# A diffusion layer on one core: the recurrence's chain as one stream of whole rows instead of two, ranked first

## The chip, the core and the metric

The kernel runs on 1 core of a Trainium2 chip. The metric is device time in microseconds (us), the median of several runs.

## What is computed

One layer over 2048 latent tokens and 256 context tokens, width 1024: modulated RMS norm, one input projection, two groups of heads side by side (neighbourhood attention and a bidirectional recurrence), an output projection, then a gated FFN. The change lies in the recurrence:

```python
def step(s, inp):
    r_t, w_t, k_t, v_t, a_t, b_t = inp
    sa = jnp.einsum('bhvk,bhk->bhv', s, a_t)
    s = s * w_t[:, :, None, :] + sa[..., None] * b_t[:, :, None, :] + v_t[..., None] * k_t[:, :, None, :]
    return s, jnp.einsum('bhvk,bhk->bhv', s, r_t)
```

It runs over 8 heads of width 64 in both directions, first over the context from a zero state, then over the latents from the state that the context leaves.

## The kernel before

Three stages follow each other. `phase1` projects all tokens and writes the recurrence's operands to DRAM. `phase2` runs attention and the recurrence side by side. `phase4` does the output projection (L1446), with the recurrence's norm and gate for each of 16 tiles of tokens just ahead of it (`TimeMixOutput.tile`, L1267 to L1283, and the transpositions L1404), and then the FFN.

In `phase2` the recurrence is cut into 36 chunks of 64 tokens per direction, two to each step `s` of 18, four to a block of two steps, so nine blocks. A pair of heads (`hp`, four of them) fills the 128 partitions, 64 each. The work of a block:

- `build` (L971) loads the operands of one step and one pair, multiplies them head by head (L1002) into one PSUM bank for each head, and spreads the result: the triangular system `lx` by ACT (L1008, two copies of 32 rows each), masked products `ga` and `gb` by DVE (L1010, L1014). Eight builds make a block. `lx` has two buffers, so the builds of block G wait for the chain of block G-2.
- `inverses` (L1042) solves the 32 systems of a block, one inverse per block: DVE transposes (L1053), POOL cuts the triangle (L1055), then DVE works through rows: single ones (L1067, L1069), then seven steps of four rows with a multiplication (L1076), a reduction (L1079) and an addition (L1080); DVE transposes back, and PE joins the halves (L1100, L1109).
- `lates` (L1019) transposes the operands that the end of a chunk needs (L1035, L1038).
- `chain` (L1160) carries the state `z` through one chunk: ACT and DVE copy it beside the loaded values (L1175, L1176), PE multiplies (L1180), ACT copies (L1184), PE multiplies by the inverse (L1188), ACT and DVE copy (L1172), PE multiplies (L1195), DVE adds the state (L1200) and scales it (L1212). From the third step on PE also forms the readout in the same bank (L1206 with 64 rows of one head, L1209 with all 128), ACT copies it (L1216) and SP stores it (L1134). There are two such chains, `g` = 0 and 1, with two pairs of heads each.

Attention runs in 64 tiles (`Attention.tiles` and `products`, L740 to L839): scores, softmax, transpositions, products with the values.

The order is made when the program is built. Every part is a generator that yields what it will occupy (`yield "run", ("ACT", 0.27)`) and what it waits for. `emit` (L862) keeps a clock for each engine and takes the part that can start first; among parts that can start at the same time a number decides, one for each stream:

```python
LATE = (60, 60, 60, -10, -10, 0, 0, 0, 60, 0)
key = (max(e[0], free.get(e[3][1][0], 0.0)), e[0] + LATE[e[1]], e[1])
emit(banks, chains(0), inverses(), chains(1), lates(0), lates(1), builds(0), builds(1), at.products(), at.tiles(),
```

The chains, the inverses and attention's tiles stand at 60. A scheduler then moves single instructions on each engine; `Run` (L48) pins a group of products to each other so that nothing comes between.

Of the kernel before, what the change touches and what calls it, by code (L numbers as in the profile page):

```python
# [93 lines left out]
def phase1(k):  # L94

    tc, nc, I = k.tc, k.nc, k.I
    with ExitStack() as ctx:
# [295 lines left out]
        def work_build(ops, hp, t0):  # L393
# [4 lines left out]
            for dd in range(2):  # L398
# [19 lines left out]
                nc.gpsimd.tensor_copy(k.pc[:, s0:s0 + 2, hp // 2, :, 2 * dd + hp % 2],  # L418
# [428 lines left out]
NU = 17  # L847
# [10 lines left out]
LATE = (60, 60, 60, -10, -10, 0, 0, 0, 60, 0)  # L858
# [53 lines left out]
def phase2(k):  # L912
# [4 lines left out]
    with ExitStack() as ctx:  # L917
# [9 lines left out]
        pch = [ps[6 + g].tile([P, 2, 4, 64], F32, name=f"pch{g}") for g in range(2)]  # L927
# [43 lines left out]
        def build(s, hp, w):  # L971
# [3 lines left out]
            if G > 1:  # L975
                yield "wait", ("chain", 2 * G - 3, 0), ("chain", 2 * G - 3, 1)
            if 4 * s + hp >= NU:
                yield "wait", ("chain", (4 * s + hp - NU) // 4, (4 * s + hp - NU) % 4 // 2)
# [16 lines left out]
            N = 128 if s > 1 else 64  # L995
            for h in range(2):
                z = []
                yield "get", z, 1
                yield "run", ("PE", 1.0)
                gp = z[0].rearrange("p (j t) -> p j t", j=4)  # L1000
                for j in range(4):
                    nc.tensor.matmul(gp[:, j, 0:N], bk[H[h], j], u.ga[H[h], h:3:2 - h, j, :] if s > 1 else  # L1002
                                     u.ga[H[h], h, j, :], start=True, stop=True)
                yield "run", ("ACT", -0.43), ("DVE", -0.34)
                ko = H[1 - h]
                for i in range(2):
# [12 lines left out]
        def lates(g):  # L1019

            for m in range(2 * NS):
                s, c = divmod(m, 2)
                if m > 1:
                    yield "wait", ("chunk", m - 2, g)
# [17 lines left out]
        def inverses():  # L1042
# [3 lines left out]
            for s in range(NS // 2):  # L1046
# [3 lines left out]
                lv = lu[:, :, 0:32]  # L1050
                x = cp.tile([P, 32, 32], F32, tag="lu", name="lu")
# [9 lines left out]
                red = cp.tile([P, 256], F32, tag="xt", name="red")  # L1061
# [74 lines left out]
        def chains(g):  # L1136

            z = ch.tile([P, 2, 2, 64], F32, tag=f"z{g}", name="z0", bufs=2)
            nc.gpsimd.memset(z, 0.0)
            if g:  # L1140
                load_v(0)
                yield "post", ("values", 0)
            yield "run", ("DMA", 2.2)
            for s in range(NS):
                yield "wait", ("inv", s // 2, 2 * g + 1)
                us = [U.pop((s, 2 * g + q)) for q in range(2)]
                for c in range(2):
                    m = 2 * s + c
                    yield "wait", ("values", m), ("late", m, g)
                    if g and m + 1 < 2 * NS:  # L1150
                        load_v(m + 1)
                        yield "post", ("values", m + 1)
                    z = yield from chain(s, c, g, z, us)
                    yield "post", ("chunk", m, g)
                yield "post", ("chain", s, g)

        dq = [(dd, q) for dd in range(2) for q in range(2)]
        kept = []

        def chain(s, c, g, z, us):  # L1160
            lx, j0 = LX[s // 2], 4 * (s % 2)
            zv = ZV[2 * s + c]
            tt = TT_.pop((2 * s + c, g))
            rp, up_ = pch[g][:, 0], pch[g][:, 1]
            gs = slice(P * g, P * g + P)

            def slot(h, dd, q):
                return zv[:, h, dd, P * g + 64 * q:P * g + 64 * q + 64]

            def keep():  # L1170
                for h, copy in ((0, nc.scalar.copy), (1, nc.vector.tensor_copy)):
                    copy(zv[H[h], h, :, gs], up_[H[h]].rearrange("p (d q) n -> p d (q n)", d=2))  # L1172

            yield "run", ("ACT", 0.27), ("DVE", 0.2)
# [521 lines left out]
```

## Time and profile before

| | us |
|---|---|
| median of 3 runs (3614.16 to 3624.52) | 3618.38 |
| the profiled execution | 3615.05 |
| its span | 3613.3 |
| PE busy in the span | 3433.7 (95%) |
| DVE, ACT, POOL busy | 2469.6, 1536.3, 1056.3 |

The span is the time from the first instruction to the last; the profiled execution's own time has 1.75 us around it. Busy is the time in which at least one instruction of the engine ran. `phase2` lies at 899 to 1988 us of the span. Products of fp32 operands have two records each in the trace.

### The profile page before, as it was taken

The numbers are of one execution on the slowest core, as the hardware profiler recorded it, in microseconds if no ns is written. First come the engines' busy times: TensorE is split into PE (matmuls) and PEld (weight loads), VectorE is DVE, ScalarE is ACT, GpSimd is POOL, SyncE is SP. The second block draws the span as 40 slices with busy tenths as digits, with TensorE's granted clock in tenths as the row PEclk, the third lists the DMA queues.
The fourth block names the chain that finished last, engine by engine and source line by source line (L and its number), as shares of the span: only waits on it lengthen the run. The fifth ranks groups of instructions, "written<-read, shape, count | busy, mean of one in ns | idle before, by whom it ended". The sixth has DMA issues, their size and how long they took to land. (4 is left out here: it accounts for less than half of the span.)

```text
span 3613.3 us, 66769 instructions
## 1 busy us (share of the span) xinstructions
PE 3433.7 (95%) x25202; PEld 2910.8 (81%) x25202; DVE 2469.6 (68%) x4570; ACT 1536.3 (43%) x3502; POOL 1056.3 (29%) x975
## 2 busy tenths in 40 slices
PE   7899999999889999999888999999899999899999
PEld 5787878889767677777676887888799999799998
DVE  7658786772675776667666674444877778777776
ACT  4524343442556566655433454323333334333332
POOL 3425543552000000000013243233433334433332
PEclk8999999999789899999866999999999999999999
DMA  7546666554544454444335455233422222412222
GB/s 238 158 146 201 188 185 190 166 165 123 160 121 129 117 145 140 124 132 123 93 91 154 141 193 170 94 96 102 140 65 70 71 70 72 162 62 71 71 70 68
DMA packets 461858, 458.52 MB, mean 127 GB/s; under 512 B 56656, under 2 KB 381664, under 8 KB 461536
## 3 DMA queue, kind: packets, MB, share of 16 engines
q1 hardware_dynamic: 461536, 454.25, 41.8%
q8 instruction: 199, 3.26, 0.4%
q14 instruction: 123, 1.01, 0.1%
HBM read 346.37 MB, written 107.75 MB: 126 GB/s over the span
## 5 line engine op out<-in xcount | busy, mean ns | idle before, releaser
L1317 ACT ACTIVATE w<-raw 128x512 fp32r<-128x512 f32 x440 | 270.4, 628 | 496.5 <-PE acc L1606 188.5
L1526 PE MATMUL acc<-ua,w 128*128 128x384 f32 x2464 | 469.1, 336 | 8.5 <-DVE h L1611 3.3
L1606 PE MATMUL acc<-w,fh 128*128 128x512 f32 x1408 | 437.5, 395 | 20.7 <-ACT fh L1317 8.4
L1318 DVE TENSOR_TENSOR w<-raw,w 128x512 fp32r<-128x512 f32 x308 | 280.5, 914 | 245.2 <-ACT w L1317 122.0
L1526 PEld LDWEIGHTS acc<-ua,w 128*128 128x128 f32 x2464 | 433.3, 189 | 11.8 <-DVE h L1611 3.7
L219 PE MATMUL acc<-u,wh 128*128 128x512 f32 (+3 forms) x1120 | 349.6, 392 | 11.7 <-ACT wh L209 5.6
L1606 PEld LDWEIGHTS acc<-w,fh 128*128 128x128 f32 x1408 | 267.2, 191 | 82.0 <-ACT fh L1317 10.2
L503 PE MATMUL acc<-wt,u 128*128 128x256 f32 x2496 | 320.8, 287 | 6.3 <-DVE sh L257 3.4
L503 PEld LDWEIGHTS acc<-wt,u 128*128 128x128 f32 x2496 | 307.4, 193 | 13.9 <-issue 5.5
L1597 POOL TENSOR_TENSOR raw<-raw,gate 128x512 f32<-128x512 f32 x132 | 179.6, 1370 | 415.7 <-DMA raw<-in_w_dram 356.2
L1606 PE MATMUL acc<-w,fl 128*128 128x512 f32 x704 | 270.5, 393 | 0.0
L1318 POOL TENSOR_TENSOR w<-raw,w 128x512 fp32r<-128x512 f32 x132 | 188.5, 1428 | 273.2 <-PE acc L1526 57.9
L219 PEld LDWEIGHTS acc<-u,wh 128*128 128x128 f32 (+1 forms) x1120 | 207.6, 193 | 58.1 <-issue 6.8
L1526 PE MATMUL acc<-ux,w 128*128 128x384 f32 x1232 | 252.0, 334 | 0.3 <-DVE w L1318 0.3
L1508 PE MATMUL acc<-ua,w 128*128 128x512 f32 x1056 | 241.7, 389 | 1.7 <-POOL w L1318 0.8
L1508 PEld LDWEIGHTS acc<-ua,w 128*128 128x128 f32 x1056 | 198.0, 188 | 43.4 <-POOL w L1318 1.3
L219 PE MATMUL acc<-u,wl 128*128 128x512 f32 (+3 forms) x560 | 218.4, 390 | 2.0 <-DVE wl L210 1.8
L1526 PEld LDWEIGHTS acc<-ux,w 128*128 128x128 f32 x1232 | 216.8, 188 | 1.6 <-DVE w L1318 1.3
L1002 PE MATMUL bank<-ga,bk 64*128 64x128 f32 (+1 forms) x1152 | 188.5, 314 | 8.4 <-DVE gb L1014 4.3
L1611 DVE TENSOR_TENSOR h<-h,acc 128x512 f32<-128x512 f32 x192 | 126.2, 683 | 101.3 <-PE acc L1606 101.0
L1002 PEld LDWEIGHTS bank<-ga,bk 64*128 64x128 f32 x1152 | 159.8, 213 | 30.0 <-issue 13.1
L1518 DVE TENSOR_TENSOR t<-acc,t 128x384 f32<-128x384 f32 x308 | 169.7, 551 | 13.9 <-PE acc L1526 7.3
(252 smaller groups left out, 6900.7 us busy)
## 6 DMA issues: line engine op xcount, KB each, us to landing
raw<-in_w_dram SPq DMA_DIRECT2D x132, 512.0 KB
raw<-in_w_dram SPq DMA_DIRECT2D x132, 256.0 KB
wada<-in_w_ada_dram SPq DMA_DIRECT2D x96, 256.0 KB
d_b<-bk SPq DMA_DIRECT2D x72, 256.0 KB
bkl<-d_b SPq DMA_DIRECT2D x144, 128.0 KB
bk<-d_b SPq DMA_DIRECT2D x72, 256.0 KB
d_b<-ar SPq DMA_DIRECT2D x136, 128.0 KB
xt<-in_x_dram SPq DMA_DIRECT2D x32, 512.0 KB
```

The lines of the kernel that those rows point to most:

```text
L219: nc.tensor.matmul(acc[:m, :n], a_[:, kk % 4, :m], b_[b][:, kk, :], start=(i == 0), stop=(i == 23))
L503: nc.tensor.matmul(acc[:, 256 * e:256 * e + 256], a_[b][:, kk, (j + e) * P:(j + e + 1) * P], ws[kk][:, h, :], start=(i == 0), stop=(i == 23))
L1002: nc.tensor.matmul(gp[:, j, 0:N], bk[H[h], j], u.ga[H[h], h:3:2 - h, j, :] if s > 1 else u.ga[H[h], h, j, :], start=True, stop=True)
L1317: nc.scalar.activation(hl[0], v, AF.Copy)
L1318: eng.tensor_tensor(hl[1], v, hl[0].bitcast(F32), op=sub)
L1508: nc.tensor.matmul(acc, hl[wi][:, kk, :], u[ui][:, 4 * hf + kk, :], start=q == 0, stop=q == 23)
L1518: vadd = lambda o, x, y: nc.vector.tensor_tensor(o, x, y, op=add)
L1526: nc.tensor.matmul(acc, w[wi][:, kk, :], u[i][ui][:, kk, :], start=q == 0, stop=q == 11)
L1597: nc.gpsimd.tensor_tensor(raw, raw, g2[:, o], op=ALU.mult)
L1606: nc.tensor.matmul(acc, a_[:, f, ts], w2[f][:, hl, :], start=(i == 0), stop=(i == 6 * np_ - 1))
L1611: nc.vector.tensor_tensor(hs[j][:, o], hs[j][:, o], acc, op=add)
```

## The change

- One `chains()` in place of two: every step of a chunk handles all four pairs of heads. The copies, the addition and the scaling are 512 elements wide instead of 256, `rp` and `up` are one PSUM bank each, and every group of products has 16 of them, pinned by `Run` with the two heads alternating.
- In the readout, POOL copies the state into `zp`, whose other half stays zero, so that the products of L1206 (now L1218) span 128 rows like those of L1209 (now L1222).
- A build takes two banks at once and alternates the heads. ACT copies 64 whole rows into `lx`; POOL moves half of them by 32 columns ahead of the inverse (L1054).
- In the inverse's seven steps the products are laid out by row, and two additions of halves take the place of the reduction (now L1078 to L1083).
- `LATE`: the chain and the inverses stand at 0 now, attention's tiles at 60. 16 unit buffers instead of 17. `pc` is laid out for whole rows.

```diff
-                nc.gpsimd.tensor_copy(k.pc[:, s0:s0 + 2, hp // 2, :, 2 * dd + hp % 2],
+                nc.gpsimd.tensor_copy(k.pc[:, s0:s0 + 2, :, dd, hp],
...
-NU = 17
+NU = 16
...
-LATE = (60, 60, 60, -10, -10, 0, 0, 0, 60, 0)
+LATE = (0, 0, -10, -10, 0, 0, 0, 60, 0)
...
-        pch = [ps[6 + g].tile([P, 2, 4, 64], F32, name=f"pch{g}") for g in range(2)]
+        rp, up_ = (ps[6 + i].tile([P, 8, 64], F32, name=n) for i, n in enumerate(("rp", "up")))
...
             N = 128 if s > 1 else 64
+            z = []
+            yield "get", z, 2
+            yield "run", ("PE", 1.0)
+            gp = [v.rearrange("p (j t) -> p j t", j=4) for v in z]
+            run = Run(k)
+            for j in range(4):
+                for h in range(2):
+                    with run.next():
+                        run.last = nc.tensor.matmul(gp[h][:, j, 0:N], bk[H[h], j], u.ga[H[h], h:3:2 - h, j, :] if s > 1
+                                                    else u.ga[H[h], h, j, :], start=True, stop=True).ins
+            dc = "p (d c) t -> p d c t"
             for h in range(2):
-                z = []
-                yield "get", z, 1
-                yield "run", ("PE", 1.0)
-                gp = z[0].rearrange("p (j t) -> p j t", j=4)
-                for j in range(4):
-                    nc.tensor.matmul(gp[:, j, 0:N], bk[H[h], j], u.ga[H[h], h:3:2 - h, j, :] if s > 1 else
-                                     u.ga[H[h], h, j, :], start=True, stop=True)
-                yield "run", ("ACT", -0.43), ("DVE", -0.34)
+                yield "run", ("ACT", -0.45), ("DVE", -0.34)
                 ko = H[1 - h]
-                for i in range(2):
-                    p0 = slice(64 * h + 32 * i, 64 * h + 32 * i + 32)
-                    nc.scalar.activation(lx[p0, hp, j0:j0 + 4, 0:64 - 32 * i], gp[p0, :, 32 * i:64], AF.Copy)
-                dc = "p (d c) t -> p d c t"
-                nc.vector.tensor_tensor(u.ga[ko, h].rearrange(dc, d=2), gp[ko, :, 0:64].rearrange(dc, d=2),
+                nc.scalar.activation(lx[H[h], hp, j0:j0 + 4, :], gp[h][H[h], :, 0:64], AF.Copy)
+                nc.vector.tensor_tensor(u.ga[ko, h].rearrange(dc, d=2), gp[h][ko, :, 0:64].rearrange(dc, d=2),
                                         maskS[ko, :, None, :].to_broadcast([64, 2, 2, 64]), op=ALU.mult)
                 if s > 1:
                     yield "run", ("DVE", -0.34)
-                    nc.vector.tensor_tensor(u.gb[:, h].rearrange(dc, d=2), gp[:, :, 64:128].rearrange(dc, d=2),
+                    nc.vector.tensor_tensor(u.gb[:, h].rearrange(dc, d=2), gp[h][:, :, 64:128].rearrange(dc, d=2),
                                             maskI[:, h, :, None, :].to_broadcast([P, 2, 2, 64]), op=ALU.mult)
-                yield "put", z[0]
+                yield "put", z[h]
...
+                for h in range(2):
+                    p0 = slice(64 * h + 32, 64 * h + 64)
+                    nc.gpsimd.tensor_copy(lu[p0, :, 0:32], lu[p0, :, 32:64])
...
-                    yield "run", ("DVE", 0.2 + 9 * m * n / 960)
-                    tv = tmp[:, :4 * m * n].rearrange("p (a b c) -> p a b c", a=m, c=4)
-                    rv = red[:, :m * n].rearrange("p (a b) -> p a b", a=m)
-                    nc.vector.tensor_tensor(tv, x[:, 0:m, None, q:q + 4].to_broadcast([P, m, n, 4]),
-                                            x[:, q:q + 4, q:32].rearrange("p c b -> p b c")[:, None].to_broadcast(
-                                                [P, m, n, 4]), op=ALU.mult)
-                    nc.vector.tensor_reduce(rv, tv, axis=AX.X, op=ALU.add)
-                    nc.vector.tensor_tensor(x[:, 0:m, q:32], x[:, 0:m, q:32], rv, op=ALU.add)
+                    yield "run", ("DVE", 0.25 + 8 * m * n / 960)
+                    tv = tmp[:, :4 * m * n].rearrange("p (c a b) -> p a c b", c=4, a=m)
+                    nc.vector.tensor_tensor(tv, x[:, 0:m, q:q + 4, None].to_broadcast([P, m, 4, n]),
+                                            x[:, None, q:q + 4, q:32].to_broadcast([P, m, 4, n]), op=ALU.mult)
+                    half = lambda i, k: tmp[:, i * m * n:(i + k) * m * n]
+                    nc.vector.tensor_tensor(half(0, 2), half(0, 2), half(2, 2), op=ALU.add)
+                    nc.vector.tensor_tensor(half(0, 1), half(0, 1), half(1, 1), op=ALU.add)
+                    nc.vector.tensor_tensor(x[:, 0:m, q:32], x[:, 0:m, q:32],
+                                            half(0, 1).rearrange("p (a b) -> p a b", a=m), op=ALU.add)
...
+        zp = ch.tile([P, 2, 2, 4, 64], F32, name="zp")
+        nc.gpsimd.memset(zp, 0.0)
...
+            yield "run", ("ACT", 0.75), ("DVE", 0.65)
+            nc.scalar.activation(zv[H[0], 0], zf[H[0]], AF.Copy)
+            nc.vector.tensor_copy(zv[H[1], 1], zf[H[1]])
+            if s > 1:
+                for h in range(2):
+                    nc.gpsimd.tensor_copy(zp[H[h], h], z[H[h]])
+            yield "run", ("PE", 1.0)
+            run = Run(k)
...
             for i, (dd, q) in enumerate(dq):
                 for h in range(2):
-                    nc.tensor.matmul(rp[H[h], i, :], us[q].ga[:, h, 2 * dd + c, :], slot(h, dd, q),
-                                     start=True, stop=True)
-            yield "run", ("ACT", 0.27)
-            rs = ch.tile([P, 4, 64], F32, tag=f"rs{g}", name="rs")
+                    with run.next():
+                        run.last = nc.tensor.matmul(rp[H[h], i, :], us[q].ga[:, h, 2 * dd + c, :], slot(h, dd, q),
+                                                    start=True, stop=True).ins
+            yield "run", ("ACT", 0.6)
+            rs = ch.tile([P, 8, 64], F32, tag="rs", name="rs")
             nc.scalar.activation(rs, rp, AF.Copy)
...
-                yield "run", ("PE", -1.15)
+                yield "run", ("PE", -1.9)
+                run = Run(k)
                 for i, (dd, q) in enumerate(dq):
                     for h in range(2):
-                        nc.tensor.matmul(up_[H[h], i, :], us[q].ga[H[h], 2, 2 * dd + c, :], z[H[h], dd, q, :],
-                                         start=True, stop=False)
+                        with run.next():
+                            run.last = nc.tensor.matmul(up_[H[h], i, :], us[q].ga[:, 2, 2 * dd + c, :],
+                                                        zp[:, h, dd, q, :], start=True, stop=False).ins
                     for h in range(2):
-                        nc.tensor.matmul(up_[H[h], i, :], us[q].gb[:, h, 2 * dd + c, :], slot(h, dd, q),
-                                         start=False, stop=True)
-            yield "run", ("DVE", 0.34)
-            nc.vector.tensor_tensor(z2v, z2v, k.pc[:, s, g, c, :, None].to_broadcast([P, 4, 64]), op=ALU.mult)
+                        with run.next():
+                            run.last = nc.tensor.matmul(up_[H[h], i, :], us[q].gb[:, h, 2 * dd + c, :],
+                                                        slot(h, dd, q), start=False, stop=True).ins
+            yield "run", ("DVE", 0.65)
+            nc.vector.tensor_tensor(z2v, z2v, k.pc[:, s, c].rearrange("p d q -> p (d q)")[:, :, None].to_broadcast(
+                [P, 8, 64]), op=ALU.mult)
             if s > 1:
-                yield "run", ("ACT", -0.54)
+                yield "run", ("ACT", -1.2)
                 for h in range(2):
-                    nc.scalar.copy(zv[H[h], h, :, gs], up_[H[h]].rearrange("p (d q) n -> p d (q n)", d=2))
-                kept.append(2 * s + c)
-                if kept.count(2 * s + c) == 2:
-                    store_y(2 * s + c)
+                    nc.scalar.copy(zv[H[h], h], upf[H[h]])
+                store_y(2 * s + c)
...
-        emit(banks, chains(0), inverses(), chains(1), lates(0), lates(1), builds(0), builds(1), at.products(), at.tiles(),
+        emit(banks, chains(), inverses(), lates(0), lates(1), builds(0), builds(1), at.products(), at.tiles(),
```

**PE, the readout of one chunk** (`z`/`zp` the state, `ga`, `gb` and `tt` the operands, `zv` the values). Before:

```order
L1195 MATMUL pch_9729<-zv,tt 64x64 x8
L1195 MATMUL pch_9730<-zv,tt 64x64 x8
L1206 MATMUL pch_9729<-z_20721,ga_9775 64x64 x2
L1209 MATMUL pch_9729<-zv,gb_9776 64x64 x2
L1206 MATMUL pch_9729<-z_20721,ga_9777 64x64 x2
```

Now:

```order
L1205 MATMUL rp<-zv,tt 64x64 x16
L1218 MATMUL up<-zp,ga_9762 64x64 x2
L1222 MATMUL up<-zv,gb_9763 64x64 x2
L1218 MATMUL up<-zp,ga_9764 64x64 x2
L1222 MATMUL up<-zv,gb_9765 64x64 x2
```

The two groups of 8 have become one of 16. The readout's rows look alike, but L1206 has tiles of 64 rows and 64 columns and L1209 of 128 and 64, while L1218 and L1222 both have 128 and 64. Counted over `phase2`, the shape of the tile changes 1428 times from one product to the next before, and 651 times now.

**PE, builds beside the chain and the last attention tile.** Before, some 20 rows into the last builds:

```order
L1002 MATMUL bank_9727<-ga_9751,bk 128x128 x3
L1188 MATMUL pch_9729<-rs,lx 64x64 x8
L1002 MATMUL bank_9727<-ga_9751,bk 128x128
L1002 MATMUL bank_9728<-ga_9753,bk 128x128 x4
L1206 MATMUL pch_9730<-z_19619,ga_9763 64x64 x2
L1209 MATMUL pch_9730<-zv,gb_9764 64x64 x2
```

Now, around the last of attention's 64 transpositions (L836):

```order
L829 MATMUL sx_9780<-pr,vc 64x128 x4
L1195 MATMUL up<-rs,lx 64x64 x16
L1004 MATMUL bank_9725<-ga_9748,bk 128x128
L836 MATMUL sx_9781<-ident,oT 128x128
L1004 MATMUL bank_9724<-ga_9748,bk 128x128
L1004 MATMUL bank_9725<-ga_9748,bk 128x128
L1004 MATMUL bank_9724<-ga_9748,bk 128x128
L1004 MATMUL bank_9725<-ga_9748,bk 128x128
L1004 MATMUL bank_9724<-ga_9748,bk 128x128
```

A build's products came four at a time from one head; now each row is of the other head's bank. At the last L836, 28 of the 36 groups L1205 have been issued; before, 24 of the 36 chunks had their L1195.

**PE, the end of `phase2`.** Before (L1404 and L1267 belong to the tiles of the output stage):

```order
L1035 MATMUL bank_9727<-ident,bkl 128x128 x2
L1404 MATMUL mtp<-ident,mx 128x128 x4
L1267 MATMUL g<-gup,gd 128x512
L1180 MATMUL pch_9730<-zv,ga_9779 64x64 x2
L1180 MATMUL pch_9730<-zv,ga_9747 64x64 x2
L1180 MATMUL pch_9730<-zv,ga_9779 64x64 x2
L1180 MATMUL pch_9730<-zv,ga_9747 64x64 x2
L1188 MATMUL pch_9729<-rs,lx 64x64 x8
L1267 MATMUL g<-gup,gd 128x512
L1188 MATMUL pch_9730<-rs,lx 64x64 x8
```

Now:

```order
L1222 MATMUL up<-zv,gb_9759 64x64 x2
L1218 MATMUL up<-zp,ga_9760 64x64 x2
L1222 MATMUL up<-zv,gb_9761 64x64 x2
L1416 MATMUL mtp<-ident,mx 128x128 x4
L1458 MATMUL acc<-wo_20857,mh 128x512 x4
L1279 MATMUL g<-gup,gd 128x512
L1458 MATMUL acc<-wo_20857,ml 128x512
```

Before, L1267 stood six times and L1404 24 times ahead of the projection's first product; now L1416 stands there four times and L1279 not at all.

## Rows read from the trace of the kernel before

**Rows 1.** The four stretches; busy us of each engine (x instructions), granted PE clock
```profile
core 0: us, PE busy (x) PEld busy (x) DVE busy (x) ACT busy (x) POOL busy (x), PEclk, DMA share, GB/s
899.00:1100.00 201.00, 174.05 (x1794) 138.51 (x1795) 135.46 (x328) 110.23 (x318) 6.88 (x8) 0.80 0.49 138
1100.00:1745.00 645.00, 621.01 (x7613) 474.49 (x7614) 428.97 (x1093) 386.62 (x1122) 15.93 (x15) 0.93 0.45 127
1745.00:1988.00 243.00, 206.48 (x2744) 163.44 (x2742) 162.66 (x284) 91.98 (x221) 43.67 (x30) 0.71 0.42 119
1988.00:2200.00 212.00, 211.19 (x1012) 171.09 (x1012) 134.66 (x217) 106.42 (x219) 68.59 (x56) 0.99 0.49 160
```

**Rows 2.** PE's timeline: start us, us, line and tile, records
```profile
1507.59 0.69 PE L1180 MATMUL pch<-zv,ga 128*64 128x64 f32 x16
1508.11 0.28 PE L1195 MATMUL pch<-zv,tt 128*64 128x64 f32 x2
...
1508.69 0.48 PE L740 MATMUL sx<-kc,q 64*128 64x256 f32 x1
1508.69 0.59 PE L740 MATMUL sw<-ks,q 64*128 64x384 f32 x1
```

**Rows 3.** PE's timeline, builds and readout products
```profile
1853.54 1.71 PE L1002 MATMUL bank<-ga,bk 64*128 64x128 f32 x16
1855.18 0.69 PE L1180 MATMUL pch<-zv,ga 128*64 128x64 f32 x16
...
1857.43 0.33 PE L1206 MATMUL pch<-z,ga 64*64 64x64 f32 x4
1857.70 0.34 PE L1209 MATMUL pch<-zv,gb 128*64 128x64 f32 x4
1857.96 0.33 PE L1206 MATMUL pch<-z,ga 64*64 64x64 f32 x4
```

**Rows 4.** Lines: count, ns min/median/max, first and last start us
```profile
L1053 DVE STREAM_TRANSPOSE lu<-lx x9: 2075/2137/2174, 944.7 to 1862.7; 128x1024 f32<-128x1024 f32 x9
L1109 PE MATMUL bank<-lx,fs x1152: 191/191/258, 1016.8 to 1926.2; 32*32 32x32 f32 x192
L1200 DVE TENSOR_TENSOR z<-pch,z x72: 376/424/427, 1040.1 to 1984.8; 128x256 f32<-128x256 f32 x72
L836 PE MATMUL sx<-ident,oT x64: 272/328/473, 940.9 to 1750.4; 128*128 128x128 f32 x64
```

**Rows 5.** Groups by line and shape: busy us, mean ns | idle before
```profile
L1008 ACT ACTIVATE lx<-bank 32x128 f32<-32x128 f32 x144 | 38.8, 270 | 1.7
L1175 ACT ACTIVATE zv<-z 64x256 f32<-64x256 f32 x72 | 29.9, 416 | 55.2 <-DVE z L1212 36.1 <-DMA d_y<-zv 13.8 <-DVE st L776 2.5
L1038 ACT ACTIVATE tt<-bank 128x512 f32<-128x512 f32 x72 | 42.7, 595 | 30.7 <-PE bank L1035 15.1 <-PE pch L1195 15.1
L1076 DVE TENSOR_TENSOR xtmp<-lu 128x960 f32<-128x960 f32 x18 | 33.1, 1837 | 0.2
L1079 DVE TENSOR_REDUCE red<-xtmp 128x240 f32<-128x960 f32 x18 | 20.6, 1147 | 0.2
L1611 DVE TENSOR_TENSOR h<-h,acc 128x512 f32<-128x512 f32 x192 | 126.2, 683 | 101.3 <-PE acc L1606 101.0
```

**Rows 6.** PE's timeline, a group of both streams at the half clock
```profile
1963.96 1.97 PE L1188 MATMUL pch<-rs,lx 64*64 64x64 f32 x32
```

**Rows 7.** SP's timeline: the DMA issues of a chunk
```profile
1520.58 2.86 SPq L1134 DMA_DIRECT2D d_y<-zv  x4
...
1524.99 2.39 SPq L1126 DMA_DIRECT2D zv<-d_vs  x4
```

**Rows 8.** Groups by line and shape on POOL
```profile
L339 POOL COPY sq<-rho 128x512 f32<-128x512 f32 x16 | 11.3, 707 | 0.6
```

**Rows 9.** DVE's timeline, end of one attention tile and of the fourth after
```profile
1218.24 0.17 DVE L803 RECIPROCAL st<-st 128x2 f32<-128x2 f32 x1
...
1256.66 0.17 DVE L803 RECIPROCAL st<-st 128x2 f32<-128x2 f32 x1
```

More of the change, by code (lines that the diff above doesn't have):

```diff
@@ L975, in build @@
             if G > 1:
-                yield "wait", ("chain", 2 * G - 3, 0), ("chain", 2 * G - 3, 1)
+                yield "wait", ("chain", 2 * G - 3)
             if 4 * s + hp >= NU:
-                yield "wait", ("chain", (4 * s + hp - NU) // 4, (4 * s + hp - NU) % 4 // 2)
+                yield "wait", ("chain", (4 * s + hp - NU) // 4)
             if G not in LX:
@@ L1023, in lates @@
                 if m > 1:
-                    yield "wait", ("chunk", m - 2, g)
+                    yield "wait", ("chunk", m - 2)
                 bk = bl.tile([P, 2, 2, P], F32, tag="bkl", name="bkl")
@@ L1060, in inverses @@
                 tmp = cp.tile([P, 1024], F32, tag="xT", name="xtmp")
-                red = cp.tile([P, 256], F32, tag="xt", name="red")
                 for q in range(1, 4):
@@ L1134, in store_y, with chains @@
                     nc.sync.dma_start(out=k.d_y[dd][t0:t0 + 64, 256 * h:256 * h + 256], in_=zv[H[h], h, dd, :])
-        def chains(g):
-            z = ch.tile([P, 2, 2, 64], F32, tag=f"z{g}", name="z0", bufs=2)
+        zp = ch.tile([P, 2, 2, 4, 64], F32, name="zp")
+        nc.gpsimd.memset(zp, 0.0)
+        def chains():
+            z = ch.tile([P, 2, 4, 64], F32, tag="z", name="z0", bufs=2)
             nc.gpsimd.memset(z, 0.0)
-            if g:
-                load_v(0)
-                yield "post", ("values", 0)
+            load_v(0)
@@ L1143, in chains @@
             yield "run", ("DMA", 2.2)
             for s in range(NS):
-                yield "wait", ("inv", s // 2, 2 * g + 1)
-                us = [U.pop((s, 2 * g + q)) for q in range(2)]
+                yield "wait", ("inv", s // 2, 3)
+                us = [U.pop((s, hp)) for hp in range(4)]
                 for c in range(2):
                     m = 2 * s + c
-                    yield "wait", ("values", m), ("late", m, g)
-                    if g and m + 1 < 2 * NS:
+                    yield "wait", ("late", m, 0), ("late", m, 1)
+                    if m + 1 < 2 * NS:
@@ L1151, in chains @@
                         load_v(m + 1)
[L1152 to L1160, printed above, removed]
+                    z = yield from chain(s, c, z, us)
+                    yield "post", ("chunk", m)
+                yield "post", ("chain", s)
@@ L1161, in chain @@
+        dq = [(dd, q) for dd in range(2) for q in range(4)]
+        def chain(s, c, z, us):
             lx, j0 = LX[s // 2], 4 * (s % 2)
             zv = ZV[2 * s + c]
-            tt = TT_.pop((2 * s + c, g))
-            rp, up_ = pch[g][:, 0], pch[g][:, 1]
-            gs = slice(P * g, P * g + P)
+            tt = [TT_.pop((2 * s + c, g)) for g in range(2)]
+            zf = z.rearrange("p d q n -> p d (q n)")
+            upf = up_.rearrange("p (d q) n -> p d (q n)", d=2)
             def slot(h, dd, q):
-                return zv[:, h, dd, P * g + 64 * q:P * g + 64 * q + 64]
@@ L1170, in keep @@
[L1170 to L1174, printed above, removed]
-            nc.scalar.activation(zv[H[0], 0, :, gs], z[H[0]].rearrange("p d q n -> p d (q n)"), AF.Copy)
-            nc.vector.tensor_copy(zv[H[1], 1, :, gs], z[H[1]].rearrange("p d q n -> p d (q n)"))
-            yield "run", ("PE", 0.57)
+                return zv[:, h, dd, 64 * q:64 * q + 64]
@@ L1182, in chain @@
-            yield "run", ("ACT", 0.27)
-            rs = ch.tile([P, 4, 64], F32, tag=f"rs{g}", name="rs")
+                    with run.next():
[3 more added lines that the diff above has]
+            rs = ch.tile([P, 8, 64], F32, tag="rs", name="rs")
             nc.scalar.activation(rs, rp, AF.Copy)
-            yield "run", ("PE", 0.57)
+            yield "run", ("PE", 1.0)
@@ L1186, in chain @@
+            run = Run(k)
             for i, (dd, q) in enumerate(dq):
                 for h in range(2):
-                    nc.tensor.matmul(up_[H[h], i, :], lx[H[h], 2 * g + q, j0 + 2 * dd + c, :], rs[H[h], i, :],
-                                     start=True, stop=True)
-            yield "run", ("ACT", 0.27), ("DVE", 0.33)
-            keep()
-            yield "run", ("PE", 0.57)
+                    with run.next():
+                        run.last = nc.tensor.matmul(up_[H[h], i, :], lx[H[h], q, j0 + 2 * dd + c, :], rs[H[h], i, :],
+                                                    start=True, stop=True).ins
@@ L1193, in chain @@
+            yield "run", ("ACT", 0.6), ("DVE", 0.6)
+            nc.scalar.copy(zv[H[0], 0], upf[H[0]])
+            nc.vector.tensor_copy(zv[H[1], 1], upf[H[1]])
+            yield "run", ("PE", 1.0)
+            run = Run(k)
             for i, (dd, q) in enumerate(dq):
                 for h in range(2):
-                    nc.tensor.matmul(rp[H[h], i, :], tt[:, q, dd, H[h]], slot(h, dd, q),
-                                     start=True, stop=True)
-            yield "run", ("DVE", 0.34)
@@ L1198, in chain @@
-            z2 = ch.tile([P, 2, 2, 64], F32, tag=f"z{g}", name="z2", bufs=2)
+                    with run.next():
+                        run.last = nc.tensor.matmul(rp[H[h], i, :], tt[q // 2][:, q % 2, dd, H[h]], slot(h, dd, q),
+                                                    start=True, stop=True).ins
+            yield "run", ("DVE", 0.65)
+            z2 = ch.tile([P, 2, 4, 64], F32, tag="z", name="z2", bufs=2)
             z2v = z2.rearrange("p d q n -> p (d q) n")
```

5 lines of the change are left out of this document (4 added, 1 removed).

## The prediction

> **What bounds the kernel now.** The windows come first [rows 1]. The middle of the program (phase2) lasts from 899 to 1988 us and has three parts. Until 1100 it fills up. From 1100 to 1745 attention runs beside the recurrence: PE is busy 621 of 645 us at a granted clock of 0.93, DVE 429, ACT 387, so PE ends the waits there. From 1745 to 1988 the recurrence is alone: PE busy 206 of 243 us at 0.71, no engine full, so a chain of dependent steps sets the pace. Then the output projection, 212 us with PE busy 211. The order of reading was windows, then PE's timeline for prices, then the lines of DVE and ACT for the widths.
>
> The trace shows two records for each fp32 product of the program, so I price records.
> - Alternating heads: 16 records of L1180 start at 1507.59 and the next group starts at 1508.11, 0.0325 us each [rows 2].
> - The readout alternates L1206 (64 rows) and L1209 (128 rows): four of one start 0.27 and 0.26 us after four of the other, so eight records take 0.53 [rows 3].
> - A build's products (L1002) stay on one half of the rows: 16 records from 1853.54 to 1855.18, 0.1025 each [rows 3].
> - That products on different row halves overlap is seen at 1508.69, where two L740 rows start at once [rows 2].
>
> **PE work removed.**
> 1. Readout: the two streams of a chunk hold 64 records, eight groups of eight, 8 x 0.53 = 4.2 us. After, 64 records of one tile shape cost 64 x 0.0325 = 2.1. Over 32 chunks 68 us are saved. (L1206 grows from 64 rows to 128 with a zero half; it gets no more columns, and the 128-row L1180 costs 0.0325 as it is, so this is free.)
> 2. Builds: 1152 records x 0.1025 = 118 us; with the heads alternating on two row halves and two banks, half of that if they overlap fully, nothing if they don't. I take 55 by the L740 rows.
> 3. Other changes of tile shape: the built programs hold 1428 of them before and 651 after, and some 490 of the difference is the readout, already counted. The remaining 290 cost at least nothing and at most (0.53 - 0.26) / 2 = 0.135 us each; I take 0.12, 34 us.
>
> Sum 157 us of PE at full clock. Part of it falls into the stretch bound by PE: 20 of the 32 readouts, seven of nine blocks of builds and three quarters of the switches, 43 + 43 + 26 = 112. But the new order puts 28 instead of 24 chunks ahead of the last attention tile, four chunks of some 7 us PE (three groups of 32 records, readout, transposes): 28 back. Net 84.
>
> **The same stretch by the chain.** Nine inverses start between 944.7 and 1862.7, one per 114.8 us, two per 229.6 [rows 4]; in both orders every second inverse stands inside the chain's run and every other one exposed. The exposed stretch is the rest of the builds (eight at 1.64 us of PE and their loads, an estimate of 20 us) and 63.5 us of inverse (L1053 at 1862.7 to L1109 at 1926.2 [rows 4]), 84 us. Eight chunks cost (229.6 - 84) / 8 = 18.2 us each now.
>
> A chunk alone, after: ACT copy 0.6, product group, ACT copy 0.6, product group, copy 0.68, product group, add 0.68, multiply 0.68. The 512-wide ACT copy is bounded by 0.42 (256 wide, L1175) and 0.60 (512 wide, L1038), the DVE ones by L1611, 0.68 [rows 5]. A group of 32 records is 1.26 us at full clock (32 x 0.0325 + one latency of 0.22) and 1.97 at half [rows 6]. Eight hand-offs at about 0.15 add 1.2. Sum 8.2 us at full clock, 10.4 at half. Beside attention it queues on three engines; SP too: its issues take about 0.6 us each, four stores 2.86 and four loads 2.39 [rows 7], and a chunk with its two builds and one attention tile has some 20 of them, 12 us. Between 12 and 18.2 I take 14, nearer to SP's floor since the chain now stands first. Two blocks: 8 x 14 + 84 = 196. The chain's first sum is at 1040 [rows 4] and I leave it at 1035; three pairs and four chunks of 11 later it is 1667, where attention ends too (1750 before [rows 4]). **-80 us**, as by PE.
>
> **The tail.** Eight chunks and one inverse are left after the last tile, before twelve chunks and most of two inverses. Chunks at 11 (the clock was 0.71 here). The inverse loses DVE time: its 960-wide multiplications take 1837 ns with strided operands, a reduction of the same width 1147 [rows 5]. Priced like that all seven steps save 3.9 us; two halving adds replace each reduction at the same cost. It also no longer shares DVE with the output stage, and two POOL copies come ahead of it (at most 0.71 each, L339 [rows 8]); 45 instead of 63.5. Tail: 44 + 45 + 44 = 133 against 243, **-110 us**.
>
> **What comes back.** Before, six tiles of the time-mix output (L1267, L1404) ran on engines left idle by the chain. Now none stands ahead of its end, so the first waits out its own DVE and POOL steps there. Between 0 and 13 us (a tile's pace, 212 / 16) plus a us of PE for each of six tiles; I take **+15**.
>
> Costed at nothing: the build's two copies on ACT become one (38.8 us of L1008 in all [rows 5], on an engine that is 60% busy); 16 unit buffers instead of 17, since the two chunk-block buffers of lx already hold the builds to two blocks. The new POOL copies (zp, two per chunk, at most 0.71 each [rows 8]) have three product groups to hide in; if POOL stood behind a waiting select, PE would wait in the readout. Phase 1 and the FFN keep their instructions.
>
> Sum: -80 - 110 + 15 = -175. The profiled execution took 3615.05 (span 3613.3), 3.3 under the median of the three runs: **3440 us**.
>
> **A rule against it.** PE's clock is 0.93 where PE is 96% busy, 0.80 where it is 87%, 0.71 where it is 85% [rows 1], so emptying PE slows it. The Trainium skill, "TensorE: Matmul & The Clock Gate", Part 1, calls the half clock the default that activity has to lift; by that rule the PE saving is partly repaid and the first rival's 3510 stands instead of 3440; the trace agrees with the direction.
>
> **Rivals.**
> - **The clock takes PE's share back.** PE's work falls to 537 us at 0.93; at 0.80, as before 1100 [rows 1], that is 624, so the attention stretch gains 20 us; the tail 100. With +15: 3510. For it: the rows just named. Against: a lower clock makes PE busier, and inside the chain's run PE stays full. Chance 0.2.
> - **Attention's own pace.** Where the chain paused, four tiles took 38.4 us, 9.6 each [rows 9]. At that pace 64 tiles end near 1550: -200, so 3320. Against: DVE is already at 67%. Chance 0.12.
> - **Slower: one stream has nothing to hide its hand-offs.** Two streams now cover each other's copies. If every one of eight hand-offs finds two or three attention instructions of 0.6 us ahead of it, a chunk takes 24 us: 276 per pair, +46 x 3.5 = +163; tail 8 x 16 + 45, -70; +15: 3723. It breaks even near 21 us a chunk. For it: engines are in order and busy. Against: the order ranks the chain first. Chance 0.08.
> - **No difference** (0.03): a chunk near 21 us. That the change doesn't do what it says is ruled out by the order.
>
> **Numbers.** Forecast 3440, chance 0.57; the rest of the rivals as above. Its neighbours: nothing in the attention stretch leaves 3520, builds that don't overlap about 3480, a chunk of 12 us 3390. The range 3360 to 3560 leaves out slower, same and half of the fast rival. A measurement tells 0.3% (11 us) from no change: faster 0.89, same 0.03, slower 0.08.
>
> **What would show it.** L1218 and L1222 at 0.0325 us a record; L1004 near 0.05; the last attention transposition near 1670 and the projection's start near 1800; a granted clock of at least 0.85 in the attention stretch. Wrong: a clock near 0.7 there, chunks over 18 us, or PE waiting on zp.

## The result and the profile after

| | before | after |
|---|---|---|
| median, us | 3617.47 (4 runs) | 3530.32 (4 runs, 3522.23 to 3533.25) |
| ratio | | 0.9753, 95% interval 0.9731 to 0.9775 |
| profiled execution / its span | 3615.05 / 3613.3 | 3522.23 / 3520.5 |
| PE, DVE busy in the span | 3433.7, 2469.6 | 3239.0, 2396.8 |
| projection's first product starts | 1988.3 | 1888.7 |

From profile to profile the change gave 92.8 us where 175 were forecast (the profiled execution is the shortest of the four). The median lies inside the range, 90 us above the forecast. The four stretches of [rows 1], moved to where they now end:

```profile
core 0: us, PE busy (x) PEld busy (x) DVE busy (x) ACT busy (x) POOL busy (x), PEclk, DMA share, GB/s
899.00:1100.00 201.00, 165.59 (x1918) 126.05 (x1920) 130.25 (x334) 101.06 (x279) 12.56 (x14) 0.82 0.50 144
1100.00:1750.00 650.00, 562.81 (x8517) 448.95 (x8516) 437.46 (x1122) 364.89 (x974) 63.38 (x78) 0.91 0.48 136
1750.00:1888.00 138.00, 75.81 (x1689) 67.72 (x1685) 70.92 (x121) 47.50 (x83) 14.08 (x19) 0.76 0.42 118
1888.00:2102.00 214.00, 210.79 (x993) 168.90 (x994) 151.03 (x261) 103.92 (x209) 97.22 (x79) 0.98 0.55 181
```

The stretch with attention kept its length (650 us, 645 before). PE was idle in 24 us of it and is now idle in 87. All the gain is in the third stretch: 138 us, 243 before. Three lines of the trace (count, ns min/median/max, first and last start), which answer to [rows 4]:

```profile
L1057 DVE STREAM_TRANSPOSE lu<-lx x9: 2104/2131/2186, 971.2 to 1790.4; 128x1024 f32<-128x1024 f32 x9
...
L1210 DVE TENSOR_TENSOR z<-rp,z x36: 664/691/693, 1039.0 to 1873.7; 128x512 f32<-128x512 f32 x36
...
L836 PE MATMUL sx<-ident,oT x64: 272/328/421, 925.6 to 1752.5; 128*128 128x128 f32 x64
```

Attention ends where it did (1752.5, before 1750.4), but with 28 chunks done instead of 24; the chain's last sum (L1210, one for each chunk) is 111 us earlier. The chunks come in runs of eight with a gap after each. Two runs (1257 to 1370, 1470 to 1591) and the gaps behind them:

```profile
1257.00:1370.00 113.00, 105.24 (x1862) 86.61 (x1861) 70.04 (x186) 72.81 (x194) 10.89 (x16) 0.97 0.59 161
1370.00:1470.00 100.00, 78.42 (x965) 61.04 (x964) 76.82 (x193) 49.61 (x134) 9.77 (x10) 0.85 0.42 124
1470.00:1591.00 121.00, 111.39 (x1914) 91.07 (x1912) 71.06 (x189) 76.17 (x202) 11.53 (x16) 0.97 0.58 163
1591.00:1688.00 97.00, 83.48 (x977) 60.61 (x978) 76.25 (x202) 50.34 (x141) 10.06 (x10) 0.89 0.38 109
```

In a run PE is full (92 to 93% busy at a clock of 0.97) and a chunk takes 16 to 17 us. In a gap nothing is full: PE 78 to 86% at 0.85 to 0.89, DVE 77 to 79%. The starts of L1004, L1057 and L1210 give the order of a pair of blocks: fourth chunk of a run (sum at 1302), then the eight builds of the next block (1310 to 1382), its inverse (1397), the next run's first sum (1470), and three chunks more (1520): 95 + 73 + 50 = 218 us round the loop. The other block's builds and inverse lie beside it.

### The profile page after: what moved, and what is told of

It is laid out like the page before. It is cut to its first block, busy times and chain, and to the rows that moved or that the text cites. A ratio compares the mean times of both kernels' runs of the same rounds, so it can differ in the third digit from the quotient of the medians.

```text
span 3520.5 us, 66352 instructions
## 1 busy us (share of the span) xinstructions
PE 3239.0 (92%) x25202; PEld 2775.8 (79%) x25202; DVE 2396.8 (68%) x4489; ACT 1465.8 (42%) x3186; POOL 1101.2 (31%) x1057
## 5 line engine op out<-in xcount | busy, mean ns | idle before, releaser
L1330 DVE TENSOR_TENSOR w<-raw,w 128x512 fp32r<-128x512 f32 x308 | 273.3, 891 | 247.0 <-ACT w L1329 120.0
L1179 POOL COPY zp<-z 64x512 f32<-64x512 f32 x64 | 41.4, 647 | 453.4 <-PE up L1218 293.7
L1330 POOL TENSOR_TENSOR w<-s,w 128x512 fp32r<-128x512 f32 x88 | 131.6, 1496 | 152.5 <-PE acc L1538 56.6
```

Of the source, the lines that this page charges most:

```text
L1179: nc.gpsimd.tensor_copy(zp[H[h], h], z[H[h]])
L1330: eng.tensor_tensor(hl[1], v, hl[0].bitcast(F32), op=sub)
```

## Experiments

Ratios are to runs of the kernel before on the same chip; "gain" is (1 - ratio) x 3617.5. The last three columns are from each profiled execution: the chain's last sum, the last attention transposition (L836), the projection's first product.

| | ratio (95%) | gain, us | chain | attention | projection |
|---|---|---|---|---|---|
| before | 1 | 0 | 1984.8 | 1750.4 | 1988.3 |
| after | 0.9753 (0.9731 to 0.9775) | 89 | 1873.7 | 1752.5 | 1888.7 |
| e1 before, builds alternate | 1.0023 (1.0006 to 1.0040) | -8 | 2001.5 | 1717.1 | 2006.4 |
| e2 before, new inverse steps | 0.9954 (0.9935 to 0.9973) | 17 | 1969.8 | 1776.8 | 1974.7 |
| e3 after, old readout | 0.9950 (0.9924 to 0.9975) | 18 | 1934.0 | 1798.1 | 1953.2 |
| e4 after, builds ahead | 0.9664 (0.9639 to 0.9688) | 122 | 1841.8 | 1759.7 | 1857.4 |
| e5 after, old rank | 0.9807 (0.9778 to 0.9837) | 70 | 1892.5 | 1599.8 | 1907.8 |
| e6 e4, lx kept | 0.9615 (0.9587 to 0.9642) | 139 | 1812.8 | 1784.7 | 1829.1 |
| e7 after, shorter inverse | 0.9565 (0.9539 to 0.9591) | 157 | 1804.1 | 1688.2 | 1819.3 |
| e8 after, no attention | 0.9343 (0.9302 to 0.9384) | 238 | 1727.4 | | 1742.7 |
| e9 after, old builds | 0.9706 (0.9683 to 0.9729) | 106 | 1794.4 | 1881.7 | 1882.7 |
| e10 after, old inverse steps | 0.9794 (0.9779 to 0.9808) | 75 | 1887.0 | 1757.0 | 1902.2 |
| e11 before, other rank | 1.0173 (1.0135 to 1.0212) | -63 | 1876.1 | 2041.4 | 2042.5 |
| e12 e6, POOL in the inverse | 0.9557 (0.9538 to 0.9577) | 160 | 1777.4 | 1801.8 | 1802.9 |

The projection starts 1 us after attention or 3.5 to 19 us after the chain's last sum, whichever is later; what follows takes 1620 to 1644 us in all of them. So a run's time is read from its two ends. (The profiled executions of e1 and e9 lie 14 and 13 us above the medians of their runs.)

**e1, the builds alone.** In `build` of the kernel before, each product as in the change:

```
-                yield "get", z, 1
+            yield "get", z, 2
```

> The kernel before with one part of the change alone: the builds write the two heads into two banks, in alternation. Theory (PE bounds the attention stretch of before, 96% busy): L1002 falls from 0.1025 to about 0.05 us a record, 55 us of PE, of which the forecast put 43 into that stretch: 3575, attention's last tile near 1705. Rival (the chain's loop of builds, inverse and chunks sets the pace there, PE only fills it): 3610 to 3617 with PE idler, or some us slower, since a build now holds both banks.

At full clock L1002's records follow each other in 0.074 us instead of 0.122, so PE was relieved as forecast, and attention ended 33 us earlier. The chain ended 17 us later, and the chain sets the end. The rival's second half held; whether the banks are the reason is not shown, since the products are now also pinned by `Run` and the plan reckons one PE step for a build instead of two.

**e2, the inverse alone.** The seven steps with halving additions, in the kernel before.

> The kernel before with another part alone: the inverse's seven steps on whole rows with two halving additions. Theory (exposed inverses are on the path): seven steps 4 to 8 us shorter, five exposed inverses, so 20 to 40 us: 3585. Rival (the inverse loses its time to the attention's DVE work ahead of it, not to its own length): at most 10 us, 3608 or more.

17 us: between the two.

**e3, the readout as before.**

```
-                        run.last = nc.tensor.matmul(up_[H[h], i, :], us[q].ga[:, 2, 2 * dd + c, :],
-                                                    zp[:, h, dd, q, :], start=True, stop=False).ins
+                        run.last = nc.tensor.matmul(up_[H[h], i, :], us[q].ga[H[h], 2, 2 * dd + c, :],
+                                                    z[H[h], dd, q, :], start=True, stop=False).ins
```

> The changed kernel with the state's half of the readout on 64 rows of z again, as before (8 records of 0.53 us a chunk where 0.0325 each now), and no copies to zp. Theory (PE is full inside the chain's runs, 93% at a clock of 0.97): 2 us a chunk come back in 28 chunks, the runs of eight grow by 16 us: 3580, attention's end near 1800. Rival (the PE saving went into idle time): 3530 to 3540.

71 us of the 89 go, more than the theory asked. PE's two lines of the readout here, against [rows 3] and the changed kernel's L1218 and L1222 below:

```profile
L1217 PE MATMUL up<-zv,gb 128*64 128x64 f32 x1024 | 94.5, 261 | 0.0
L1213 PE MATMUL up<-z,ga 64*64 64x64 f32 x1024 | 94.4, 260 | 0.0
```

The pair grows from 216 to 228 us, the two runs shown above by 15 and 10 us (113 to 128, 121 to 131), and attention ends 46 us later: in the runs PE time is time. The Trainium skill, "TensorEngine Tiling (Array Packing)", Key Properties, says that a change of the tiling mode drains the engine; the rows agree in that such a change has a price, and show no drain as such: at full clock a record takes 0.066 us where the two row counts alternate, 0.0305 where all have 128.

**e4, builds and inverses ahead.**

```
-LATE = (0, 0, -10, -10, 0, 0, 0, 60, 0)
+LATE = (0, -60, -10, -10, -60, -60, 0, 60, 0)
```

> The changed kernel with builds and inverses ranked 60 us ahead of the chain. Theory (the pair of 216 us is a loop: fourth chunk of a run, then the next block's eight builds, 80 us, then its inverse, 57 us, then the next run's first four chunks): builds end earlier in the run, the stretch without chunks falls from 98 us by 10 to 30, three and a half times: 3470 to 3500. Rival (attention's own pace, 64 tiles, ends at 1750 whatever the chain does): 3530, or slower by the chunks that fall behind.

33 us over the change. From the fourth chunk to the inverse it is 75 to 95 us (93 to 98 in the change), and the distance between the runs falls from 97 to 100 us to 63 to 74; attention ends 7 us later. Part of that comes back inside the runs, where from the second run on the fourth and fifth sums are 30 to 42 us apart (15 to 20 in the change), so the pair falls by 20 us, from 216 to 196. The theory's loop held.

**e5, the old rank.** LATE starts with 60, 60.

> The changed kernel with chain and inverses ranked like the attention, 60, as in the kernel before; the single stream, zp, the alternating builds and the row operations stay. Theory (the loop of chunks, builds and inverse sets the end, so its place in the order counts): attention ends 50 to 100 us earlier, the chain later, 3550 to 3590. Rival (the readout's 68 us of PE are the whole gain and the rank is worth nothing): 3530 within 10.

The rank is worth 19 us: between the two. Attention ends 153 us earlier and the chain 19 us later, so ranking moves much work for little time.

**e6, lx kept.** On top of e4:

```
-            if G > 1:
-                yield "wait", ("chain", 2 * G - 3)
...
-                LX[G] = lp[G % 2].tile([P, 4, 8, 64], F32, tag="lx", name="lx")
+                LX[G] = LX[G - 2] if G > 1 else lp[G % 2].tile([P, 4, 8, 64], F32, tag="lx", name="lx")
```

> The changed kernel with builds and inverses ranked 60 us ahead (as in the experiment with 3487), and the lx buffer kept instead of allocated anew for each block, so that the first four builds of a block wait for the chain's first two chunks of two blocks before and no longer for all four. Theory (the loop through builds and inverse): the stretch without chunks, 69 us with builds ahead, falls by 15 to 30, three times: 3420 to 3450. Rival (PE and DVE are full by then, the builds only push chunks and attention back): 3475 to 3500.

The step from e4 is 17 us where the theory wanted 38 or more. The chain is 29 us earlier, but attention is now at 1784.7: the two ends close up, and what the chain gains attention pays for.

**e7, a shorter inverse.** `for q in (4, 8, 24, 28)`.

> The changed kernel without three of the inverse's seven steps (columns 12, 16 and 20, some 8 us of DVE; the inverse is left incomplete). Theory (the exposed inverse is on the loop): 8 to 12 us in each of five exposed inverses: 3475 to 3495. Rival (attention's own pace or PE sets the stretch up to 1750): only the tail's inverse shows, 3515 to 3525.

68 us over the change for 8 us of DVE in each inverse: more than the theory asked, and the rival is out (attention ends at 1688).

**e8, the chain alone.**

> The changed kernel without the attention's scores, softmax and products (zeros are stored for its output; its operands are still prepared): the chain alone. Theory (sharing the engines doubles the loop): a pair is 4 chunks of 10.3, 20 us of builds and an inverse of 45, 106 us against 216; four and a half pairs end the chain near 1520, 3170. Rival (the loop waits on its own loads, hand-offs and banks): a pair of 160 or more, 3400.

The rival's number held: a pair takes 160 to 164 us (first sums of runs at 1059, 1219, 1383, 1547). Most of the theory's miss is in its builds: in the pair from 1219 it is 57 us from the fourth chunk to the inverse, where 20 were taken, then 55 to the next sum (45 taken) and 52 to the fourth (41). Which of loads, hand-offs and banks the builds wait for was not separated. Two runs and their gaps:

```profile
1059.00:1144.00 85.00, 62.52 (x1286) 55.20 (x1284) 49.20 (x91) 31.86 (x60) 7.11 (x10) 0.77 0.39 112
1144.00:1219.00 75.00, 45.65 (x601) 38.63 (x598) 53.64 (x104) 17.09 (x37) 9.79 (x10) 0.57 0.29 87
1219.00:1317.00 98.00, 70.06 (x1528) 62.87 (x1526) 51.84 (x93) 37.59 (x70) 10.91 (x16) 0.83 0.39 113
1317.00:1383.00 66.00, 41.61 (x606) 35.49 (x602) 52.91 (x101) 16.30 (x35) 9.76 (x10) 0.59 0.30 91
```

Alone, a chunk in a run takes 12 to 14 us (85 / 7, 98 / 7), not the tail's 8 to 10.5: from the second run on, the first three intervals between sums, which lie beside the second inverse, are 15 to 20 us, the others 9 to 16. All of attention costs the changed kernel 149 us beyond this loop.

**e9, the builds as before.** Each head's products in one go, with one bank of their own.

> The changed kernel with the builds' products of the two heads one after the other, each with a bank of its own, as before (one copy each stays). Theory (PE is no longer the bound outside the chain's runs, and a build that needs one bank at a time starts earlier): 1152 records go back to 0.1025 us, 55 us of PE, mostly in the stretch where PE is 80% busy: 3525 to 3545. Rival (the PE time of the builds is on the loop, eight builds of 1.64 instead of 0.8 us): 7 us per pair and more in the runs, 3560 to 3580.

Both missed: it is 17 us faster than the change, with PE busy 75 us longer. The chain ends 79 us earlier, at 1794.4, and attention last of all. What stands between the fourth chunk (L1210 of after at 1302, here 1246) and the next inverse (1397, here 1312), after and e9; x counts tiles:

```profile
L836 PE MATMUL sx<-ident,oT 128*128 128x128 f32 x9 | 2.9, 322 | 0.2 <-ACT oT L834 0.2
```

```profile
L836 PE MATMUL sx<-ident,oT 128*128 128x128 f32 x3 | 0.9, 290 | 0.0
```

Nine tiles of attention are issued ahead of the inverse with alternating builds, three with these, and the way from chunk to inverse is 95 us against 66 (93 to 98 against 52 to 82 over all runs). An alternating build asks for both of the two free banks at once and holds them; that this is what lets attention in first is read from the code, and no run separates it from the rest of the new order. e9 also drops the pinning by `Run` and reckons two PE steps for a build in the plan instead of one; each of these could be the reason as well.

**e10, the old inverse steps.** The counterpart of e2, in the changed kernel.

> The changed kernel with the inverse's seven steps as before (strided multiplication, reduction, addition: 20.6 us of DVE where 15.6 now). Theory (leaving out 8 us of DVE per inverse gave 78 us, so the loop returns the inverse's DVE time many times over): 5 us of DVE, 3565 to 3585. Rival (that gain came from another order that the planner found, not from the length): 3545 to 3555, the 15 us that the new steps gave in the kernel before.

15 us, close to e2's 17: the rival's amount. The old steps cost 4 us more of DVE in each inverse (19.7 for 15.7, not 20.6), some 20 on five exposed ones, so the loop gave back about as much as DVE saved, not many times over. e7's 68 for 8 us (40 by the same count) came in part with another order, in which attention ends 64 us earlier; the parts are not separated.

**e11, the other rank in the kernel before.** `LATE = (60, 60, 60, ...)` becomes `(0, -60, 0, -10, -10, -60, -60, 0, 60, 0)`.

> The kernel before with another rank alone: builds and inverses 60 us ahead, both chains 0, attention 60. Theory (a loop of chunks, builds and inverse holds the kernel before too): 30 to 50 us faster, 3560 to 3580. Rival (PE is 96% busy there, so the order only moves work about): 3595 to 3615.

Worse than either: the chain ends 109 us earlier, attention 291 later. Rank chose who waits, and PE did not stay full: from 1100 to 1700 it is 89% busy at a clock of 0.86, where it was 96% busy before, so the rival's reason does not hold either. That e4's gain needs the PE time which the readout set free is likely, but no run shows it: the kernel before also has two streams and the old builds.

**e12, rows of the inverse on POOL.** On top of e6, in each step:

```
+for eng, buf, r0, r1 in ((nc.gpsimd, tmq, 0, 4), (nc.vector, tmp, 4, m)):
```

> The version of 3471 us (builds and inverses ahead, lx kept), and in each of the inverse's seven steps the first four of the rows are worked on POOL, a third of the elements, while DVE does the others; a row's steps never need another row's result. Theory (the inverse's DVE time is on the loop): DVE falls by 4 to 5 us per inverse, 3425 to 3450. Rival (POOL is slower than the DVE rows it goes beside, or both slow each other down): 3470 or more.

3451.49 us as run, ratio 0.9557: 71 us ahead of the change and the fastest kernel here that leaves nothing out, though the step from e6, 21 us, falls just short of what the theory asked (3451 for 3425 to 3450). DVE's time in the seven steps fell only from 15.7 to 13.6 us per inverse, since its instructions take longer with POOL beside them. The addition of 128x192 (L1084) shows it within the run: eight of its 18 lie beside a POOL instruction of these steps for over nine tenths of their length and take 0.98 us on the mean, six lie beside none and take 0.35. The changed kernel, then e12:

```profile
L1078 DVE TENSOR_TENSOR xtmp<-lu 128x768 f32<-128x768 f32 x18 | 17.1, 952 | 0.3
...
L1081 DVE TENSOR_TENSOR xtmp<-xtmp 128x384 f32<-128x384 f32 x18 | 10.0, 554 | 0.4
```

```profile
L1081 DVE TENSOR_TENSOR xtmp<-lu 128x768 f32<-128x768 f32 x18 | 18.8, 1047 | 0.2
...
L1084 DVE TENSOR_TENSOR xtmp<-xtmp 128x384 f32<-128x384 f32 x18 | 12.2, 676 | 0.2
```

**The change's 89 us, part by part:** taken out one at a time, the readout is worth 71 (e3), the rank 19 (e5), the inverse's steps 15 (e10) and the builds -17 (e9), together 88. Each of these is a difference of two ratios and uncertain by 10 to 13 us, and one at a time need not add up, so that the sum comes so close is partly chance; what the single stream itself is worth stays open, as no run took it out alone.

## Why the prediction was right in direction and half in size

- **The readout's price: right.** "0.0325 us a record": in the changed kernel's PE timeline the second of these rows starts 21 records after the first, in 0.59 us, and the mean at full clock is 0.0305. It has lines without idle time ahead, so PE does not wait on zp either.

```profile
1108.79 0.22 PE L1222 MATMUL up<-zv,gb 128*64 128x64 f32 x1
...
1109.38 0.22 PE L1222 MATMUL up<-zv,gb 128*64 128x64 f32 x1
```

```profile
L1218 PE MATMUL up<-zp,ga 128*64 128x64 f32 x1024 | 75.8, 238 | 0.0
L1222 PE MATMUL up<-zv,gb 128*64 128x64 f32 x1024 | 75.1, 237 | 0.0
```

- **The builds' saving: right by luck, their worth: wrong.** Sixteen records take 1.16 us (1.71 in [rows 3]), some 0.07 a record where about 0.05 was taken. The mean at full clock fell from 0.122 to 0.075 where the forecast had 0.1025 and 0.05: both rates were too low by about as much, so the saving of 54 us over 1152 records met the 55. In time the builds were worth -17 and -8 us (e9, e1). What the prediction costed at nothing, and did not name, is that a build now needs both banks, is pinned as one group and is planned as one step; which of these costs the time is not shown.

```profile
1349.91 1.16 PE L1004 MATMUL bank<-ga,bk 64*128 64x128 f32 x16
```

- **"Sum 157 us of PE at full clock": right.** Busy time times granted clock, from 899 to the projection, was 174 x 0.80 + 621 x 0.93 + 206 x 0.71 = 863 us and is 166 x 0.82 + 563 x 0.91 + 76 x 0.76 = 706, 157 less. By part: the readout (0.066 - 0.0305) x 2048 = 73 (68 taken), the builds 54, and so 30 for all else (34), of which some 5 only moved behind the projection's start with 20 transpositions of the output stage (four take 1.08 us).

- **"The same stretch by the chain", -80 us: this step failed.** It gave 196 us for a pair of blocks; the three pairs took 648.9 (first sums at 1039.0 and 1687.9), 216 each. The exposed stretch came out as priced (97 to 100 us from sum to sum, less one chunk: 82, forecast 84). The chunk was mis-sized: 16 to 17 us in a run for "Between 12 and 18.2 I take 14". Twelve to fourteen is what e8 shows with no attention at all on the engines; the estimate left attention nothing. It was taken from SP's issue time, but SP issues for only 82.5 of the 113 us of the run from 1257, 10.3 a chunk, while PE is busy for 105.
- **The same step misread the kernel before, so the 84 us fitted by luck.** It put the exposed stretch at 84 us "in both orders" and the chunk at 18.2. The sums of before, both streams counted, are 61, 46 and 46 us apart from run to run, and the eight chunks of a run take 154, 193 and 211 us from first to last sum, 21 to 28 each. One such gap:

```profile
1448.46 0.42 DVE L1200 TENSOR_TENSOR z<-pch,z 128x256 f32<-128x256 f32 x1
...
1494.59 0.42 DVE L1200 TENSOR_TENSOR z<-pch,z 128x256 f32<-128x256 f32 x1 [0.18 <-PE pch L1195]
```

  On the mean of three pairs the change shortened the runs from 186 to 117 us and lengthened the gaps from 51 to 99: of the 69 us that the runs gave, the gaps took back 48.
- **That the way by PE gave the same -80 was no second witness.** It held the stretch for bound by PE after the change as before. PE went from 96 to 87% busy, and the 63 us more of idle time lie mostly in the gaps, where the inverse and attention share DVE. The chain's loop, not PE's work, then set the pace.
- **Where the 89 us between forecast and measured start of the projection (1800 and 1888.7) arose:** first sum +4; three pairs +61; on to the sum of the 28th chunk +9 (52.7, three intervals, for four chunks of 11); from there to the projection +15 (148.1 for 133). This last part is 133.1 to the chain's last sum and 15.0 from it to the projection, where it was 3.5 before. Inside the 133.1 an inverse shorter than priced makes up for one interval between sums, 1841.7 to 1865.1, that is 13 us longer than the usual 10. The waits there (engine, line, waited for: us, times, longest) show ACT and DVE splitting the output weights ahead of the chain's copies:

```profile
DVE wo L1330 <- ACT wo L1329: 9.4, 4, 5.6
PEld up L1195 <- ACT rs L1189: 8.0, 1, 8.0
PE up L1195 <- ACT rs L1189: 7.8, 1, 7.8
```

- **The tail, -110: right within a tenth**, 105 by the third stretch. The chunk alone takes 8 to 10.5 us (11 taken) but for the interval just named; the stretch of the inverse is 48 from sum to sum, less one chunk some 38 (45 taken). The sizes erred both ways and cancelled. The seven steps take 15.7 us of DVE on the mean of nine for 19.8, so 4.1 saved for the 3.9 priced.
- **What comes back, +15:** 18, for another reason. From the projection's start on it was 1625.0 us and is 1631.8, 7 more; the other 11 lie ahead of it, in the 15.0 us after the last sum (3.5 before). PE waits there for a load that SP issues behind the chain's last stores, not for the tile's DVE and POOL steps:

```profile
1886.91 1.08 PE L1416 MATMUL mtp<-ident,mx 128*128 128x128 f32 x4 [11.45 <-DMA mx<-d_mix]
```

- **The clock's rival: its direction, not its size.** It asked for 0.80 in the attention stretch; 0.91 was granted there, 0.93 before: 0.97 in the two runs shown, where PE stayed full, and 0.85 to 0.89 in their gaps. In the chain alone, with PE 61 to 74% busy, it is 0.57 to 0.83. The Trainium skill's default of half clock ("TensorE: Matmul & The Clock Gate", Part 1) agrees with that, but this kernel is not emptied that far.
- **The other rivals:** attention's pace of 9.6 us a tile was reached for a few tiles (four in 37.1 us from 1299), but over all 64 it is 13.1, with DVE at 77 to 79% in the gaps; and a chunk stayed below the 21 us from which the change would have lost. The neighbour that was named for "nothing in the attention stretch", 3520, is what came.

## What to carry to other kernels

Where two streams share the engines and the next stage waits for both, PE time that is saved counts only for the one that ends last, and here it counted in the stretches in which PE is full; look in the changed order for the loop that decides the other stretches (here fourth chunk, builds, inverse) and price that. Look at the gaps as well as at the work: here shorter runs were paid for with longer gaps. What an instruction group asks for together, and how it is planned, belongs in the sum like its instructions: the alternating builds saved 54 us of PE and lost 8 and 17 us of time, perhaps by the pair of banks. And where the hand-offs have been freed of PE, rank the work that opens the next round ahead of the work of this one, which here gave 33 us, and 71 with two more steps.

## What had not been expected

DVE lost time to POOL in e12, where both work on the inverse: 952 ns became 1047 (128x768), 554 became 676 (128x384). And a PE that is busy 75 us longer ran the whole 17 us faster (e9): with an order laid down in advance, the sum of an engine's work says little about the end.
